# Output projection of a hybrid encoder layer: six of eight token groups as seven half-depth products of sums of quarters

## The chip, the cores and the metric

The kernel runs on one core of one Trainium2 chip. The metric is device microseconds of one execution. Three runs of the kernel before gave 2144.36, 2150.53 and 2152.09 us, so the median is 2150.53 us.

## The reference

One encoder layer with 2048 tokens and 1024 channels. A combined input projection feeds a gated DeltaNet and a stick-breaking attention; each branch is gated, projected up to 1024 channels and merged. What the change touches is the last line:

```python
merged = gates[..., :D_MODEL] * y_a + gates[..., D_MODEL:] * y_b      # [2048, 1024]
return x + jnp.einsum('bsd,de->bse', merged, w_out)                   # w_out: [1024, 1024]
```

All data is float32. The result is x plus a product of a 2048x1024 matrix with a 1024x1024 matrix.

## The kernel before

The program has two stages. `stage1` computes the input projection, the attention and the recurrence. `stage2` finishes the recurrence, computes the up projections (`up`, line 902) for eight groups of OG = 256 tokens, and then the output projection (`outs`, line 923) for the same eight groups.

Every product with f32r operands is made of three: each operand is split into a part `hi` (ScalarE casts it) and a rest `lo` (VectorE or GpSimd subtracts), and TensorE adds hi*hi, hi*lo and lo*hi (`mm3`, line 892). One matmul multiplies a stationary block of 128 channels by 128 tokens with 128 channels by 512 output columns.

`up(g)` leaves the merged activations in DRAM: for each of eight channel blocks VectorE multiplies two PSUM halves by the gates (`yt`, line 918), GpSimd adds the two (line 919), and the SP queue stores the block into the scratch `d_m[g]` (line 920), laid out as 128 channels, 8 blocks, 256 tokens.

`outs(g)` loads the eight blocks of `d_m[g]` back (`split`, line 882: tile `ot` with four buffers, ScalarE cast on line 888, VectorE subtract on line 889) into half of the tiles `xh2` and `xl2`, where the two halves alternate by group. For each of its two rows of 128 tokens it loads x (`xt`, three buffers), and for each of two halves of the output columns it issues 24 matmuls into one PSUM bank (tile `o`, pool `po`, six banks), adds x (line 933) and stores the row (line 937). The very last row is stored in two halves (line 935). That is 96 matmuls a group and 768 in all. The weights `w_out` lie in SBUF as hi and lo: blocks 0 to 3 in the pool `wq`, blocks 4 to 7 in the former space of x's third quarter of tokens (`xh3`, `xl3`).

The pools `oq` and `po` are opened on the right side of memory beside the pools `op` and `py` of the up projections, and a scheduler orders each engine's instructions and the SP queue's transfers. TensorE's own order is that of the program, held by explicit dependencies (`pin`, line 130). Each engine and the SP queue work through their lists in order, so an instruction that waits holds up what stands behind it.

Of the kernel before, what the change touches and what calls it, by code (L numbers as in the profile page):

```python
# [18 lines left out]
P = 128  # L19
# [18 lines left out]
class Block:  # L38
    """The layer in three stages; DRAM scratch carries what a stage leaves for a later one."""

    def __init__(self, ctx, tc, ins, out):
        self.ctx, self.tc, self.nc = ctx, tc, tc.nc
        self.i = ins
        self.out = out
        dr = ctx.enter_context(tc.tile_pool(name="dr", bufs=1, space=DRAM))

        def scratch(name, n, shape):
            return [dr.tile(shape, F32, name=f"{name}{i}") for i in range(n)]

        self.d_kq = dr.tile([NC, P, NH, 2, P], F32, name="d_kq")  # L50
        self.d_kt = dr.tile([NC, P, NH, P], F32, name="d_kt")
        self.d_vn = dr.tile([NC, P, NH, P], F32, name="d_vn")
        self.d_qk = dr.tile([NC, P, NH, P], F32, name="d_qk")
        self.d_mt = dr.tile([NC, NH, P, P], F32, name="d_mt")
        self.d_tt = dr.tile([NC, NH, 2, HB, HB], F32, name="d_tt")
        self.d_za = scratch("d_za", NC, [P, NH * P])
        self.d_q = dr.tile([2, SH * SD, S], F32, name="d_q")
        self.d_k = dr.tile([2, SH * SD, S], F32, name="d_k")
        self.d_v = dr.tile([SH, P, NT, P], F32, name="d_v")
        self.d_zb = scratch("d_zb", 4, [P, S])  # L60
        self.d_g = scratch("d_g", S // OG, [P, KB, 2, OG])
        self.d_oa = dr.tile([4, P, S], F32, name="d_oa")
        self.d_ob = dr.tile([4, P, S], F32, name="d_ob")
        self.d_m = dr.tile([S // OG, P, KB, OG], F32, name="d_m")
        self.now, self.pending, self.back, self.credit, self.rate = 0, [], None, 0.0, 0.0
        self.op, self.lead = None, 0
        self.chain, self.last, self.clock, self.attended, self.zb_done = False, None, 0.0, False, 0
        self.consts()
# [35 lines left out]
    def params(self):  # L104
        """The small parameters."""
# [24 lines left out]
    def pin(self, ins):  # L130
        """Keep the tensor engine in program order."""
        if self.chain and self.last is not None:
            self.tc.add_manual_dep(ins.ins, self.last, mybir.DependencyInfo(mybir.DependencyClass.NoSync, mybir.DependencyReason.DATA), reason="order")
        self.last = ins.ins.name if self.chain else None

    def load(self, *args):
        """A load whose queue keeps program order during the first tiles."""
# [6 lines left out]
    def defer(self, steps, fn):  # L144
        """Emit fn after the matrix products of `steps` further steps."""
        self.pending.append((self.now + steps, fn))
# [9 lines left out]
    def advance(self, amount, limit=4.0):  # L156
        """Let the background work emit about `amount` us of the tensor engine's time, or what it has ready."""
# [18 lines left out]
    def drain(self):  # L176
        """All that is left of the background work."""
        while self.back is not None:
            self.advance(1e9)
            self.clock += 0.2  # L180
# [13 lines left out]
    # ---------------------------------------------------------------- stage 1  # L194
# [63 lines left out]
    def ready(self, g):  # L258
        """Have the recurrence done for tokens of the up projections' group g."""
# [13 lines left out]
    def gap(self):  # L273
        """Background work between the products of a projection; the recurrence follows the attention."""
# [58 lines left out]
    def rsq(self, pool, ssq, n, scale, eps, tag):  # L333
        """(ssq * scale + eps) ** -0.5 on n columns."""
# [7 lines left out]
    def prep_x(self, first):  # L342
        """Normalised x, transposed to channels by tokens, in two parts that f32r products carry exactly."""
# [40 lines left out]
    def mm_chan(self, w, j, tg, between=None):  # L384
        """Projection block [128 channels, 512 tokens]."""
# [10 lines left out]
    def mm_tok(self, w, t, ps, n):  # L396
        """Projection block [128 tokens, n channels]."""
# [31 lines left out]
    def decays(self):  # L429
# [14 lines left out]
        # e = exp(-|xa|) = s1 / s2, log1p(e) = 2 atanh(e / (2 + e)), e / (2 + e) = s1 / (2 s2 + s1)  # L444
# [56 lines left out]
    def qkb_store(self, qn, dst, kind, u, tp):  # L501
        """To channels by tokens, q with both gains, in two parts that f32r products carry exactly."""
# [31 lines left out]
    def conv(self, ps, b, halo):  # L534
        """Causal four-tap convolution of a block; the caller multiplies what it returns for SiLU."""
# [36 lines left out]
    def qk_tok(self, kq, tg, h):  # L572
        """Norms of q and k, k by tokens, and the decay between a chunk's tokens."""
# [95 lines left out]
    # gated delta rule: within a chunk of 128 tokens, inverses of the two diagonal blocks of 64  # L669
    def dn_solve(self):  # L670
        """Unit triangular inverses by substitution, one block to a partition.

        With b[x, i] = -m[i, x] for x < i, step j adds b[x, j] b[j, i] to b[x, i]."""
# [38 lines left out]
    def dn_states(self):  # L712
# [9 lines left out]
        def store(most=0):  # L722
            """Emit what is due, and all but `most` of the rest when its time comes."""
# [55 lines left out]
    def dn_chunk(self, c, loads, st, mo):  # L779
        """One chunk of the recurrence; k and q come without their norms, which nk, nbr and rq carry."""  # L780
# [28 lines left out]
        # rms over a head's values; o carries neither q's norm nor dk ** -0.5 yet  # L809
# [21 lines left out]
    # ---------------------------------------------------------------- stage 2  # L831
    def stage2(self):
        """The up projections follow the recurrence; then the rest."""
        NO = S // OG
        with ExitStack() as ctx:
            self.op = ctx.enter_context(self.pool("op"))
            self.py = ctx.enter_context(self.pool("py", space=PSUM))
# [19 lines left out]
            self.oq = ctx.enter_context(self.pool("oq", side="right"))  # L857
            po = ctx.enter_context(self.pool("po", bufs=6, space=PSUM, side="right"))
            while jobs:
                self.run_job(jobs)  # L860
            for g in range(NO):
                self.outs(g, self.wo, po)

    def run_job(self, jobs):
        """A piece of the first job; the next one's loads run ahead of its end."""
# [16 lines left out]
    def split(self, src, k, g):  # L882
        """[128, OG] from DRAM in two parts, one of two sets."""
# [18 lines left out]
    def up(self, g):  # L902
        """Gated sum of both up projections for OG tokens, channels by tokens."""
# [19 lines left out]
    def outs(self, g, wo, po):  # L923
        nc, op = self.nc, self.op
        m = [self.split(self.d_m[g, :, k], k, g) for k in range(KB)]
        for t in range(OG // P):
            r0 = g * OG + t * P
            xt = self.oq.tile([P, D], F32, tag="xt", name="xt", bufs=3)
            nc.sync.dma_start(xt, self.i["x"][0, r0:r0 + P])
            for c in range(2):  # L930
# [3 lines left out]
                if r0 + P == S:  # L934
                    nc.sync.dma_start(self.out[0, r0:, c * TG:c * TG + TG], xt[:, c * TG:c * TG + TG])
            if r0 + P < S:
                nc.sync.dma_start(self.out[0, r0:r0 + P], xt)

    def att_pools(self, ctx):
# [9 lines left out]
        # added to a logit, it makes the key weigh nothing and break nothing  # L949
# [4 lines left out]
    # from a tile's products to its transposes, from there to the products with v, between two tiles, in us  # L954
    LT, LP, LZ = 4.5, 2.2, 1.3

    def attention(self):
        """Stick-breaking attention: one slot is a tile of 128 queries by 512 keys (or fewer on the diagonal)."""
# [5 lines left out]
        def ready():  # L964
            """Emit what is due; the sets of buffers bound how far one kind runs ahead of another."""
# [105 lines left out]
    def att_trans(self, A, m, edge):  # L1071
        """Two tiles' weights for two blocks of keys, the later block first, keys by queries in two parts."""
# [44 lines left out]
```

## Time and profile before

| what | value |
|---|---|
| runs of the kernel | 2144.36, 2150.53, 2152.09 us (median 2150.53) |
| profiled execution, span from first to last instruction | 2144.5 us |
| TensorE busy | 2058.2 us, 96% |
| VectorE busy | 1493.9 us, 70% |
| ScalarE busy | 875.2 us, 41% |
| GpSimd busy | 969.8 us, 45% |
| output projection, first to last matmul | 1963.4 to 2140.7 us |

The page gives the profiled execution's span and no other time for it; that span lies at the fastest of the three runs and 6.0 us under their median. Busy shares are of the whole span; an engine that is lightly loaded on average can be the last to arrive in one stage.

### The profile page before, as it was taken

The page shows a single profiled execution, that of the slowest core. Times are in us where ns is not written, and L with a number is a line of the kernel's source. Part 1 is how long each engine was busy: PE and PEld are TensorE (multiplying, and loading weights), DVE is VectorE, ACT ScalarE, POOL GpSimd, SP SyncE. Part 2 cuts the span into 40 slices and gives each one's busy share as a digit, 9 for nine tenths or more (in the row PEclk, how much of TensorE's full clock was granted, in tenths as well). Part 3 has the DMA queues.
Part 4 walks back from the last instruction along what each step waited for, and adds up shares of the span by engine and source line. Part 5 has one row for each costly group of instructions (what it writes and reads, how often), then busy time and mean ns, then how long its engine had stood idle before and what let it go on. Part 6 is the DMA issues. An engine that isn't in the chain of part 4 may idle for free.

```text
span 2144.5 us, 36573 instructions
## 1 busy us (share of the span) xinstructions
PE 2058.2 (96%) x12903; PEld 1821.1 (85%) x12903; DVE 1493.9 (70%) x2899; ACT 875.2 (41%) x1695; POOL 969.8 (45%) x820
## 2 busy tenths in 40 slices
PE   7999988999999999999999999999999999999999
PEld 7988767779999988878778888888788899999887
DVE  7367778887998329898889898889854466433221
ACT  6224433422222126666666666666643321211110
POOL 4335666534443215555556655555436655521000
PEclk9999999999999999999999999999999999999999
DMA  7123332226333553333664443333337787764442
GB/s 238 63 62 94 94 104 84 84 73 125 118 114 111 151 137 105 104 113 109 159 171 128 125 117 99 107 103 104 101 107 232 221 272 220 228 183 139 152 136 82
DMA packets 279702, 282.52 MB, mean 132 GB/s; under 512 B 49440, under 2 KB 215520, under 8 KB 279392
## 3 DMA queue, kind: packets, MB, share of 16 engines
q1 hardware_dynamic: 279520, 280.19, 44.8%
q8 instruction: 103, 1.69, 0.3%
q14 instruction: 79, 0.65, 0.1%
HBM read 177.35 MB, written 102.76 MB: 131 GB/s over the span
## 4 chain that ended last, share of the span: by engine, by line
PE 59%; DVE 23%; ACT 6%; DMA 4%; issue 4%; POOL 3%; SPq 0%; ACTq 0%; POOLq 0%; DVEq 0%
PE pj L124 30%; DVE r L1065 9%; PE o L124 8%; PE y L124 6%; DVE acc L548 4%; PE av L124 4%; DVE lo L1084 3%; PE at L128 3%; PE dn L124 3%; PE z L124 3%; ACT r L1061 2%; PE tp L128 1%; DMA wraw<-in_w_in_dram 1%; DVE halo L544 1%; DVE carry L1067 1%
## 5 line engine op out<-in xcount | busy, mean ns | idle before, releaser
L1068 POOL TENSOR_TENSOR s<-s,r 128x512 f32<-128x512 f32 (+2 forms) x320 | 372.5, 1174 | 335.5 <-DVE r L1065 183.7
L124 PE MATMUL pj<-xh,whi 128*128 128x512 f32 x1024 | 420.9, 411 | 12.0 <-ACT u L542 10.1
L124 PE MATMUL pj<-xh,wlo 128*128 128x512 f32 x1024 | 405.3, 396 | 0.0
L124 PE MATMUL pj<-xl,whi 128*128 128x512 f32 x1024 | 404.7, 395 | 0.0
L1065 DVE TENSOR_TENSOR_SCAN r<-r,carry,zero 128x512 f32<-128x512 f32 x192 | 302.2, 1574 | 23.2 <-ACT r L1061 22.0
L124 PE MATMUL pj<-whi,xh 128*128 128x256 f32 (+1 forms) x1024 | 293.3, 286 | 1.0 <-ACT xh L380 1.0
L124 PE MATMUL pj<-whi,xl 128*128 128x256 f32 (+1 forms) x1024 | 289.7, 283 | 0.0
L124 PE MATMUL pj<-wlo,xh 128*128 128x256 f32 (+1 forms) x1024 | 289.5, 283 | 0.2 <-DVE wlo L330 0.2
L124 PEld LDWEIGHTS pj<-xh,whi 128*128 128x128 f32 x1024 | 194.0, 189 | 49.2 <-ACT u L542 14.9
L1061 ACT ACTIVATE r<-z 128x512 f32<-128x512 f32 (+2 forms) x320 | 171.9, 537 | 152.2 <-PE z L124 53.9
L124 PEld LDWEIGHTS pj<-xh,wlo 128*128 128x128 f32 x1024 | 193.3, 189 | 44.5
L124 PEld LDWEIGHTS pj<-xl,whi 128*128 128x128 f32 x1024 | 194.3, 190 | 32.0
L1084 DVE TENSOR_TENSOR lo<-at,hi 128x512 fp32r<-128x512 f32 (+1 forms) x288 | 183.7, 653 | 28.3 <-ACT hi L1083 27.1
L124 PEld LDWEIGHTS pj<-whi,xh 128*128 128x128 f32 x1024 | 194.1, 190 | 1.4 <-ACT xh L380 1.4
L124 PEld LDWEIGHTS pj<-wlo,xh 128*128 128x128 f32 x1024 | 194.3, 190 | 0.5 <-DVE wlo L330 0.5
L124 PEld LDWEIGHTS pj<-whi,xl 128*128 128x128 f32 x1024 | 193.9, 189 | 0.3 <-DVE xl L381 0.3
L1083 ACT CAST hi<-at 128x512 fp32r<-128x512 f32 (+1 forms) x288 | 154.3, 571 | 96.7 <-PE at L128 94.7
L124 PE MATMUL z<-kt,qt 128*128 128x512 f32 (+3 forms) x640 | 189.4, 377 | 4.2 <-ACT s L1062 2.9
L330 POOL TENSOR_TENSOR wlo<-wraw,whi 128x512 fp32r<-128x512 f32 (+2 forms) x66 | 122.4, 1854 | 112.6 <-ACT whi L329 111.7
L1062 ACT ACTIVATE s<-z 128x512 f32<-128x512 f32 (+2 forms) x320 | 171.1, 535 | 0.0
L128 PE MATMUL at<-ident,s 128*128 128x128 f32 x1088 | 156.9, 274 | 11.3 <-POOL s L1068 11.1
L124 PE MATMUL av<-lo,vt 128*128 128x256 f32 x576 | 148.4, 292 | 17.0 <-DVE r L1064 9.9
(200 smaller groups left out, 4293.5 us busy)
## 6 DMA issues: line engine op xcount, KB each, us to landing
kt<-d_k SPq DMA_DIRECT2D x160, 128.0 KB, 3.0
vt<-d_v SPq DMA_DIRECT2D x80, 256.0 KB, 3.5
xt<-in_x_dram SPq DMA_DIRECT2D x32, 512.0 KB, 3.9
qt<-d_q SPq DMA_DIRECT2D x64, 256.0 KB, 5.2
d_g<-sg SPq DMA_DIRECT2D x128, 128.0 KB, 2.5
gt<-d_g SPq DMA_DIRECT2D x64, 256.0 KB, 3.6
wraw<-in_w_in_dram SPq DMA_DIRECT2D x56, 256.0 KB, 3.2
wraw<-in_w_in_dram SPq DMA_DIRECT2D x18, 512.0 KB, 3.8
```

What stands on the lines that cost most here:

```text
L124: self.pin(self.nc.tensor.matmul(out, lhsT, rhs, **kw))
L128: self.pin(self.nc.tensor.transpose(*args))
L330: (eng or nc.gpsimd).tensor_tensor(lo[:, ks, :n], raw[:, :, :n], hi[:, ks, :n].bitcast(F32), ALU.subtract)
L544: nc.vector.tensor_copy(halo, u[:, TG:TG + 3])
L548: nc.vector.scalar_tensor_tensor(acc, u[:, k:k + TG], self.tap(k, b), acc, ALU.mult, ALU.add)
L1061: nc.scalar.activation(r[:, :w], z[:, :w], AF.Sigmoid, scale=-(SD ** -0.5))
L1062: nc.scalar.activation(s[:, :w], z[:, :w], AF.Sigmoid, scale=SD ** -0.5)
L1065: nc.vector.tensor_tensor_scan(r[:, 0:w][:, ::-1], r[:, 0:w][:, ::-1], self.zero.to_broadcast([P, w]), init, ALU.mult, ALU.add)
L1067: nc.vector.tensor_copy(carry[i], r[:, 0:1])
L1068: nc.gpsimd.tensor_mul(s[:, :w], s[:, :w], r[:, 1:w + 1])
L1083: nc.scalar.copy(hi[:, c:], flat[:, c:])
L1084: nc.vector.tensor_tensor(lo[:, c:], flat[:, c:], hi[:, c:].bitcast(F32), ALU.subtract)
```

## The change

The up projections' pools are closed before the output projection starts, and the output projection's pools (`oq`, and `po` with seven banks) are opened in their place. Groups 0 and 1 are computed as before, except that each of the two `xt` tiles has one buffer of its own and the last row is stored whole. Between them `out_sums` loads `w_out` again, a quarter of its rows at a time, and forms four combinations of its quarters, the sums `t7`, with 16 subtractions of 128x512 on GpSimd and 16 splits into hi and lo. They lie where the weights of the up projections were (`xh0`, `xl0`, `xh1`, `xl1`).

Groups 2 to 7 use `outs7`. The group's activations are a 2x2 arrangement of quarters (two rows of 128 tokens, two halves of the channels): a11, a12, a21, a22. One transfer of 1 MB brings them into the tile `m`, which has one buffer and shares it with the tile of `out_sums` (tag `raw`). GpSimd forms four combinations s1 to s4 of 128x512 (the tiles are named `s0` to `s3`). Seven products of half depth (four channel blocks, 12 matmuls of 512 columns each) take the place of eight: p1 = a11*B11, p6 = s2*T2, p7 = s3*T3, p5 = s1*T1, then a12*B21 added into p1's bank, s4*B22 added into p5's bank, and p4 = a22*T4. Every left operand is split (`halves`: a ScalarE cast and a VectorE subtract of 128x512) into one of eight slots in `xh2` and `xl2`, taken in turn. VectorE forms u2 = p6 + p1 and u3 = p7 + u2; GpSimd adds u2 to one quarter of x and u3 to two; VectorE adds p1, p5 (twice) and p4 from PSUM.

```diff
     def stage2(self):
         with ExitStack() as ctx:
-            self.op = ctx.enter_context(self.pool("op"))
-            self.py = ctx.enter_context(self.pool("py", space=PSUM))
+            rest = ExitStack()
+            self.op = rest.enter_context(self.pool("op"))
+            self.py = rest.enter_context(self.pool("py", space=PSUM))
...
-            self.oq = ctx.enter_context(self.pool("oq", side="right"))
-            po = ctx.enter_context(self.pool("po", bufs=6, space=PSUM, side="right"))
             while jobs:
                 self.run_job(jobs)
-            for g in range(NO):
-                self.outs(g, self.wo, po)
+            rest.close()
+            self.op = self.oq = ctx.enter_context(self.pool("oq"))
+            po = ctx.enter_context(self.pool("po", bufs=7, space=PSUM))
+            self.outs(0, self.wo, po)
+            t7 = self.out_sums()
+            self.outs(1, self.wo, po)
+            for g in range(2, NO):
+                self.outs7(g, self.wo, t7, po)
...
+    def halves(self, hi, lo, src):
+        self.nc.scalar.copy(hi, src)
+        self.nc.vector.tensor_tensor(lo, src, hi.bitcast(F32), ALU.subtract)
+
+    def out_sums(self):
+        nc, oq = self.nc, self.oq
+        t7 = [[None] * 4 for _ in range(4)]
+        for k in range(4):
+            raw = oq.tile([P, KB * OG], F32, tag="raw", name="raw", bufs=1)
+            for r in range(2):
+                nc.sync.dma_start(raw[:, r * D:r * D + D], self.i["w_out"][0, (k + 4 * r) * P:(k + 4 * r) * P + P])
+            b11, b12, b21, b22 = (raw[:, TG * n:TG * n + TG] for n in range(4))
+            t = [oq.tile([P, TG], F32, tag=f"s{n}", name=f"s{n}", bufs=1) for n in range(4)]
+            for o, x, y in ((t[0], b12, b11), (t[1], b22, t[0]), (t[2], b22, b12), (t[3], b21, t[1])):
+                nc.gpsimd.tensor_tensor(o, x, y, ALU.subtract)
+            for n in range(4):
+                t7[n][k] = tuple(x[n // 2][:, n % 2 * 4 + k] for x in (self.xh, self.xl))
+                self.halves(*t7[n][k], t[n])
+        return t7
+
+    def outs7(self, g, wo, t7, po):
+        nc, oq = self.nc, self.oq
+        m = oq.tile([P, KB, OG], F32, tag="raw", name="m", bufs=1)
+        nc.sync.dma_start(m, self.d_m[g])
+        a11, a12, a21, a22 = (m[:, 4 * k:4 * k + 4, r * P:r * P + P] for r in range(2) for k in range(2))
+        s1, s2, s3, s4 = (oq.tile([P, 4, P], F32, tag=f"s{n}", name=f"s{n}", bufs=1) for n in range(4))
+        for o, x, y, op in ((s1, a21, a22, ALU.add), (s2, s1, a11, ALU.subtract), (s3, a11, a21, ALU.subtract), (s4, a12, s2, ALU.subtract)):
+            nc.gpsimd.tensor_tensor(o, x, y, op)
+        xt = [oq.tile([P, D], F32, tag=f"xt{r}", name="xt", bufs=1) for r in range(2)]
...
+        def product(ps, a, b, first=True):
+            slot = self.slot
+            self.slot = (slot + 1) % KB
+            hi, lo = (x[2][:, slot].rearrange("p (k t) -> p k t", k=4) for x in (self.xh, self.xl))
+            self.halves(hi, lo, a)
+            for k in range(4):
+                for n, (u, v) in enumerate(((hi, b[k][0]), (hi, b[k][1]), (lo, b[k][0]))):
+                    self.mm(ps, u[:, k], v, start=first and k == 0 and n == 0, stop=k == 3 and n == 2, skip_group_check=not first)
...
+        product(p1, a11, quarter(0, 0))
+        nc.scalar.copy(m1, p1)
+        product(p6, s2, t7[1])
+        add(nc.vector, u2, p6, m1)
+        product(p7, s3, t7[2])
+        add(nc.vector, u3, p7, u2)
+        add(nc.gpsimd, x22, x22, u3)
+        product(p5, s1, t7[0])
+        add(nc.vector, x22, p5, x22)
+        product(p1, a12, quarter(1, 0), False)
+        add(nc.gpsimd, x12, x12, u2)
+        add(nc.vector, x11, p1, x11)
+        product(p5, s4, quarter(1, 1), False)
+        add(nc.gpsimd, x21, x21, u3)
+        add(nc.vector, x12, p5, x12)
+        nc.sync.dma_start(self.out[0, rows[0]], xt[0])
+        product(p4, a22, t7[3])
+        add(nc.vector, x21, p4, x21)
+        nc.sync.dma_start(self.out[0, rows[1]], xt[1])
```

The SP queue at the end of the last up projection, before: `d_m` is the store of a block of the up projection, `gt` the load of its gates, and `ot` the load of activations for the output projection.

```order
L911 DMA gt<-d_g_93 128x512
L887 DMA ot<-d_m 128x256
L920 DMA d_m<-yt 128x256
L887 DMA ot<-d_m 128x256 x3
...
L920 DMA d_m<-yt 128x256 x3
L887 DMA ot<-d_m 128x256
L920 DMA d_m<-yt 128x256
L887 DMA ot<-d_m 128x256 x4
L920 DMA d_m<-yt 128x256
L887 DMA ot<-d_m 128x256 x3
```

The same place now, and the rows that follow up to the first load of a group's activations in one piece (`m`); `raw` is the second load of `w_out` and `xt` is x:

```order
L916 DMA gt<-d_g_93 128x512
L925 DMA d_m<-yt 128x256 x5
L892 DMA ot<-d_m 128x256 x4
L934 DMA xt<-in_x_dram 128x1024 x2
L892 DMA ot<-d_m 128x256 x4
L953 DMA raw<-in_w_out_dram 128x1024 x2
L892 DMA ot<-d_m 128x256 x8
L953 DMA raw<-in_w_out_dram 128x1024 x2
...
L953 DMA raw<-in_w_out_dram 128x1024 x2
L939 DMA out_dram<-xt 128x1024
L967 DMA m<-d_m 128x2048
```

All loads of groups 0 and 1 moved behind the last store of the up projections; before, all eight of group 0 and five of group 1 stood ahead of it.

GpSimd in one of the later groups (before, GpSimd has nothing behind the last `yt`); `s0`, `s2`, `s1`, `s3` with m_23297 are the sums s1, s3, s2, s4 of group 4, the last row begins group 5, and `xt_23175`, `xt_23176` are the x rows of group 3, where the first of the two additions to `xt_23176` is to the quarter that p5 also goes to:

```order
L971 TENSOR_TENSOR s0_23299<-m_23297 128x512
L971 TENSOR_TENSOR s2_23301<-m_23297 128x512
L971 TENSOR_TENSOR s1_23300<-s0_23299,m_23297 128x512
L994 TENSOR_TENSOR xt_23175<-xt_23175,u2_23181 128x512
L971 TENSOR_TENSOR s3_23302<-m_23297,s1_23300 128x512
L994 TENSOR_TENSOR xt_23176<-xt_23176,u3_23182 128x512 x2
L971 TENSOR_TENSOR s0_23431<-m_23429 128x512
```

VectorE beside it, in group 3; the tile o_23231 is p5's bank, o_23179 is p1's, o_23280 is p4's:

```order
L944 TENSOR_TENSOR xl2_141<-m_23297,xh2_137 128x512
L994 TENSOR_TENSOR u2_23181<-o_23198,m1_23180 128x512
L944 TENSOR_TENSOR xl2_141<-s2_23301,xh2_137 128x512
L994 TENSOR_TENSOR u3_23182<-o_23214,u2_23181 128x512
L944 TENSOR_TENSOR xl2_141<-s1_23300,xh2_137 128x512
L944 TENSOR_TENSOR xl2_141<-s0_23299,xh2_137 128x512
L944 TENSOR_TENSOR xl2_141<-m_23297,xh2_137 128x512
L994 TENSOR_TENSOR xt_23176<-o_23231,xt_23176 128x512
L994 TENSOR_TENSOR xt_23175<-o_23179,xt_23175 128x512
L944 TENSOR_TENSOR xl2_141<-s3_23302,xh2_137 128x512
L994 TENSOR_TENSOR xt_23175<-o_23231,xt_23175 128x512
L944 TENSOR_TENSOR xl2_141<-m_23297,xh2_137 128x512
```

A group's sums and splits are made one group ahead, and the x quarter that p5 goes to gets u3 on GpSimd behind five other sums.

## Rows read from the trace of the kernel before

**Rows 1.** The chain of waits in order of time, from 1955 us: start, length, what.
```profile
1955.00 8.40 PE y L124 x70
1963.40 177.30 PE o L124 x768
2140.70 0.02 issue
2140.72 0.69 DVE xt L933
```

**Rows 2.** Busy time by stretch: length, busy of five engines, TensorE clock, DMA share, GB/s.
```profile
1985.20:2007.00 21.80, 21.80 (x96) 17.71 (x95) 5.63 (x12) 2.75 (x7) 0.00 (x0) 1.00 0.42 142
2051.00:2073.00 22.00, 22.00 (x97) 17.87 (x96) 6.04 (x13) 3.52 (x9) 0.00 (x0) 1.00 0.44 143
```

**Rows 3.** Timelines at the up projections' end: start, length, engine, what, idle before.
```profile
1942.91 0.41 ACT L888 CAST xh<-ot 128x256 fp32r<-128x256 f32 x1 [4.07 <-DMA ot<-d_m]
1963.49 0.69 DVE L918 TENSOR_TENSOR yt<-y,gt 128x512 f32<-128x512 f32 x1 [0.16 <-issue]
1964.26 0.74 POOL L919 TENSOR_TENSOR yt<-yt 128x256 f32<-128x256 f32 x1 [1.89 <-DVE yt L918]
1965.72 0.39 SPq L920 DMA_DIRECT2D d_m<-yt  x1
```

**Rows 4.** DMA issues from 1964 to 2140 us: KB each, us to landing.
```profile
out_dram<-xt SPq DMA_DIRECT2D x15, 512.0 KB, 2.7
xt<-in_x_dram SPq DMA_DIRECT2D x13, 512.0 KB, 3.3
ot<-d_m SPq DMA_DIRECT2D x49, 128.0 KB, 2.8
out_dram<-xt SPq DMA_DIRECT2D x1, 256.0 KB, 2.0
```

**Rows 5.** All loads into `ot` from 1920 to 1990 us: time to landing.
```profile
DMA to landing us min/median/max: 2.4/2.9/4.6
```

**Rows 6.** Groups by line and shape, whole span: count, busy us, mean ns, idle before.
```profile
L888 ACT CAST xh<-ot 128x256 fp32r<-128x256 f32 x128 | 49.9, 406 | 241.4 <-PE o L124 101.1 <-PE y L124 77.9 <-DMA ot<-d_ob 29.2
L879 ACT CAST woh<-raw 128x512 fp32r<-128x512 f32 x8 | 5.0, 619 | 16.9 <-DMA raw<-in_w_out_dram 15.9 <-DMA gt<-d_g 0.8
L1084 DVE TENSOR_TENSOR lo<-at,hi 128x512 fp32r<-128x512 f32 x224 | 149.4, 683 | 27.9 <-ACT hi L1083 27.1
L933 DVE TENSOR_TENSOR xt<-o,xt 128x512 f32<-128x512 f32 x32 | 22.1, 690 | 114.5 <-PE o L124 114.5
```

**Rows 7.** GpSimd groups by line and shape, whole span.
```profile
L880 POOL TENSOR_TENSOR xl<-raw,xh 128x512 fp32r<-128x512 f32 x24 | 30.5, 1282 | 9.2 <-ACT xh L879 7.8 <-DMA vn<-d_vn 1.4
L1068 POOL TENSOR_TENSOR s<-s,r 128x512 f32<-128x512 f32 x224 | 300.2, 1350 | 257.1 <-DVE r L1065 123.3 <-DVE r L1064 40.6 <-ACT s L1062 26.1
L330 POOL TENSOR_TENSOR wlo<-wraw,whi 128x512 fp32r<-128x512 f32 x40 | 57.4, 1435 | 73.0 <-ACT whi L329 72.7
```

**Rows 8.** Timeline of VectorE and GpSimd where they meet, from 1937 us.
```profile
1937.79 1.98 DVE L889 TENSOR_TENSOR xl<-ot,xh 128x256 fp32r<-128x256 f32 x4
1937.82 0.99 POOL L919 TENSOR_TENSOR yt<-yt 128x256 f32<-128x256 f32 x1 [2.14 <-DVE yt L918]
1940.70 0.73 POOL L919 TENSOR_TENSOR yt<-yt 128x256 f32<-128x256 f32 x1 [1.89 <-DVE yt L918]
```

**Rows 9.** TensorE around a wait for VectorE: timeline rows, then two stretches.
```profile
1862.39 0.28 PE L124 MATMUL y<-xh,xl 128*128 128x256 f32 x1
1865.24 0.39 PE L124 MATMUL y<-xh,xh 128*128 128x256 f32 x1 [2.58 <-DVE yt L918]
...
1866.00:1869.40 3.40, 3.40 (x18) 3.40 (x18) 3.22 (x4) 2.11 (x6) 3.40 (x4) 0.51 0.82 255
1869.40:1871.00 1.60, 1.60 (x15) 1.60 (x15) 1.60 (x2) 0.84 (x2) 1.41 (x2) 1.00 0.93 316
```

More of the change, by code (lines that the diff above doesn't have):

```diff
@@ L65, in __init__ @@
         self.now, self.pending, self.back, self.credit, self.rate = 0, [], None, 0.0, 0.0
-        self.op, self.lead = None, 0
+        self.op, self.lead, self.slot = None, 0, 0
         self.chain, self.last, self.clock, self.attended, self.zb_done = False, None, 0.0, False, 0
@@ L927, in outs @@
             r0 = g * OG + t * P
-            xt = self.oq.tile([P, D], F32, tag="xt", name="xt", bufs=3)
+            xt = self.oq.tile([P, D], F32, tag=f"xt{t}", name="xt", bufs=1)
             nc.sync.dma_start(xt, self.i["x"][0, r0:r0 + P])
@@ L933, in outs @@
                 nc.vector.tensor_tensor(xt[:, c * TG:c * TG + TG], ps, xt[:, c * TG:c * TG + TG], ALU.add)
[L934 to L937, printed above, removed]
+            nc.sync.dma_start(self.out[0, r0:r0 + P], xt)
+    def halves(self, hi, lo, src):
+        self.nc.scalar.copy(hi, src)
+        self.nc.vector.tensor_tensor(lo, src, hi.bitcast(F32), ALU.subtract)
@@ new lines, in outs7, with bank, temp @@
+    def outs7(self, g, wo, t7, po):
[7 more added lines that the diff above has]
+        xt = [oq.tile([P, D], F32, tag=f"xt{r}", name="xt", bufs=1) for r in range(2)]
+        rows = [slice(g * OG + r * P, g * OG + r * P + P) for r in range(2)]
+        for r in range(2):
+            nc.sync.dma_start(xt[r], self.i["x"][0, rows[r]])
+        (x11, x12), (x21, x22) = ((t[:, 0:TG], t[:, TG:D]) for t in xt)
+        quarter = lambda k, c: [tuple(u[:, c * TG:c * TG + TG] for u in w) for w in wo[4 * k:4 * k + 4]]
+        def product(ps, a, b, first=True):
[6 more added lines that the diff above has]
+                    self.mm(ps, u[:, k], v, start=first and k == 0 and n == 0, stop=k == 3 and n == 2, skip_group_check=not first)
+        def bank():
+            return po.tile([P, TG], F32, tag="o", name="o")
+        def temp(name):
+            return oq.tile([P, TG], F32, tag=name, name=name, bufs=1)
+        add = lambda eng, o, x, y: eng.tensor_tensor(o, x, y, ALU.add)
+        p1, m1, u2, u3 = bank(), temp("m1"), temp("u2"), temp("u3")
+        product(p1, a11, quarter(0, 0))
+        nc.scalar.copy(m1, p1)
+        p6 = bank()
+        product(p6, s2, t7[1])
+        add(nc.vector, u2, p6, m1)
+        p7 = bank()
+        product(p7, s3, t7[2])
+        add(nc.vector, u3, p7, u2)
+        add(nc.gpsimd, x22, x22, u3)
+        p5 = bank()
+        product(p5, s1, t7[0])
[7 more added lines that the diff above has]
+        nc.sync.dma_start(self.out[0, rows[0]], xt[0])
+        p4 = bank()
+        product(p4, a22, t7[3])
+        add(nc.vector, x21, p4, x21)
+        nc.sync.dma_start(self.out[0, rows[1]], xt[1])
```

## The prediction, made before the changed kernel ran

> **What bounds the kernel now.** I read the chain of waits first, because it says which engine a saved instruction must come from. From 1963.4 us to 2140.7 us it is one piece: 768 matmuls of the output projection on TensorE, with a VectorE addition behind it [rows 1]. So a matmul taken away there shortens the span by its spacing, 177.30 / 768 = 0.2309 us, as long as TensorE keeps being fed. The table by stretches says how much room the others have: in 22 us TensorE is busy throughout at full clock, VectorE for about 6, ScalarE for about 3, GpSimd not at all, and the DMA engines are at 42 to 44% [rows 2]. What the change adds goes to those engines, so the averages look harmless. What matters is order: who must finish before TensorE may go on. For that I read the timelines at the start of the stage [rows 3], the DMA landing times [rows 4, 5] and the durations of the kinds of instruction that are added [rows 6, 7].
>
> All times below are counted on the profiled execution, whose span is 2144.5 us; the median of the runs is 2150.53 us, 6.0 more, and I carry the difference over to the median. About 0.5%, 10.75 us, is what a measurement of this kernel can tell from no change.
>
> **The change part by part.**
>
> 1. *Fewer matmuls.* Six groups have 84 instead of 96: 72 x 0.2309 = 16.6 us less. The forms are the same 128x512, the weights stay in SBUF, so nothing else about a matmul changes.
>
> 2. *The way in.* Before, the activations of group 0 were split by 1945 us, long before TensorE needed them at 1963.4: the row at 1942.91 is the fifth of its eight casts [rows 3]. Now the first load stands behind the last store of the up projections. That store waits for GpSimd's last addition, which ends at 1964.26 + 0.74 = 1965.0 [rows 3]. One issue takes 0.4, so the first load is issued at 1965.4, lands 2.8 later [rows 4], and is cast in 0.41 [rows 6]: the first matmul starts at about 1968.6 instead of 1963.4, 5.2 us late. There are four buffers, so the fifth load waits for VectorE's first subtract (about 0.5, a quarter of the 1.98 in [rows 8]): issued 1969.1, ready 1972.3, while the first four blocks keep TensorE until 1968.6 + 12 x 0.2309 = 1971.4. That adds 0.9. Together **+6.1**. With the shortest and longest landing seen, 2.4 and 4.6 [rows 5], twice in a row, it is 5.3 to 9.7.
>
> 3. *The clock.* After a wait of 2.58 us at 1865 us TensorE ran at 1.2 GHz for 3.4 us: 18 matmuls took 3.40 us where at 2.4 GHz 15 took 1.60 [rows 9]; so 18 would have taken 1.9, and the loss was 1.5. A wait of 5.2 us should bring the same: **+1.6**; 0 if the low level passes while TensorE stands idle, 3.4 if it comes twice.
>
> 4. *The sums of w_out,* cover and price. Sixteen GpSimd subtractions run under groups 0 and 1. If one takes c, a round is a load of 3.3 [rows 4], 0.2 of issue and 4c, and the single buffer keeps rounds from overlapping. The first load is issued behind the eighth load of group 0, at about 1971.0. After four rounds comes group 2's 1 MB load. No row shows such a load: 128 KB lands in 2.8 and 512 KB in 3.3 [rows 4], a slope that gives 4.0, and two of 512 KB one after the other would be 6.6; I take 5, nearer the first, since the DMA engines are half idle. For c the rows of the same shape say 1.28 with little beside it, 1.35 in the attention and 1.435 for the subtraction in the projections [rows 7]. I take 1.44, as here too VectorE subtracts beside it. Then rounds end at 1971.0 + 4 x 9.26 = 2008.0, m is there at 2013.1, and the sum for p6 with its cast at 2013.1 + 3 x 1.44 + 0.62 = 2018.0. TensorE reaches p6 at 1963.4 + 6.1 + 1.6 + 192 x 0.2309 + 2.77 = 2018.2. So **0**, with 0.2 to spare; what is late next, if this gives way, is p6 itself.
>
> 5. *The wait for p5's bank in group 2.* The fifth and sixth products add into banks that VectorE and ScalarE read first. The sixth may start only when p5 has been added to x, and that addition waits for GpSimd's x + u3, which in GpSimd's list stands behind the next group's first three sums and x + u2; those wait for the next 1 MB load. Its issue needs group 2's fourth sum: 2013.1 + 4 x 1.44 = 18.9, then 0.4 + 5, five GpSimd operations 7.2 and VectorE 0.69 [rows 6]: 2032.2. TensorE wants the bank five products after 2015.4, at 2029.3: **+2.9** (0 with c = 1.28 and a fast load, 5 with c = 1.74).
>
> 6. *The ring in groups 3 to 6.* The same steps close a circle: load 5, six GpSimd operations 6c, VectorE 0.69, the sixth product 2.77, the cast of a22 0.62, two VectorE operations 1.4, issue 0.4. At c = 1.44 that is 19.5 against a group's 84 x 0.2309 = 19.4: **+0.4** over four groups. Splits (ScalarE 7 x 0.62, VectorE 13 x 0.69 a group) are made a group ahead and lie beside TensorE; without that cover each would cost 1.3 before its product.
>
> 7. *The end.* The last store is a whole row: 2.7 instead of 2.0 [rows 4], **+0.7**. The loads of x have one buffer a row now, and each waits for its row's store, 2.7 + 3.3 = 6 us into the next group, before u3 exists: nothing.
>
> Sum: -16.6 + 6.1 + 1.6 + 0 + 2.9 + 0.4 + 0.7 = -4.9 us; 2150.5 - 4.9 = **2145.6**.
>
> **Rivals.** *GpSimd sets the pace (the slower side).* In terms 4 to 6 c counts 19, 6 and 24 times: a tenth of a microsecond more in c costs 4.9 us. The gain is gone at c = 1.54, and it is slower by 10.75 from c = 1.76. For it: GpSimd's 256-column addition took 0.99 beside four VectorE subtracts from SBUF and 0.73 alone [rows 8]; the same stretch on 1.28 gives 1.74, hence -4.9 + 49 x 0.30 = +9.8, **2160**. The Trainium skill says the same of the cause: by its page "GPSIMD Engine Reference", section "Key points", GpSimd shares its SBUF interfaces with VectorE and contends with VectorE instructions that have two SBUF inputs, as all the added splits have; the rows at 1937 agree in sign. Against it: in the attention, with VectorE scanning beside it, the mean was 1.35, and the splits fill only 2.8 of some 8 us of a group's GpSimd work. Chance 0.22, of which 0.08 beyond c = 1.76.
>
> *The loads set the pace.* If 1 MB lands in 6.6, because the row stores and x loads travel with it, term 4 costs 1.4, term 5 1.6 more and the ring 6.4: +4.5, **2155**. For it: one buffer, so each load starts only when the last reader is done; against it: 42% DMA share. Chance 0.13.
>
> *The waits are mostly covered.* Shortest landing, c = 1.28, no low clock, loads of 4.0: -16.6 + 5.3 + 0.7 = -10.6, **2140**. For it: GpSimd is otherwise idle here. Against it: the way in stands in the order and can't be avoided, and the wait of 2.58 did bring the low clock. Chance 0.10, half of it beyond 0.5%.
>
> **The numbers.** The forecast, 2145.6, has 0.55 and its own range is 2142 to 2151. The rivals reach from 2140 to 2160; leaving out the upper part of the first, the lower edge of the last and some of the scatter of 8 us between runs, I give 2139.5 to 2159. Faster by over 0.5%: half of the last rival and the forecast's lower edge, 0.08. Slower by over 0.5%: 0.09, the first rival from c = 1.76 on and a little for the loads. Same: 0.83.
>
> **What would show it.** Right: 696 matmuls of the output projection; TensorE idle for 5 to 6 us from 1963.4, ended by a load or cast of group 0, and a granted clock of half for some 3 us behind it; p6 of group 2 waiting under 2 us; VectorE's addition of p5 waiting for GpSimd in group 2; groups 3 to 7 at 19.4 to 19.6 us each. Wrong: groups of 20 us or more with TensorE waiting for VectorE each time (the ring, then c or the landing says which), a start of group 2 later than 2020 us, or no wait at all at 1963 us.

## The result and the profile after the change

The changed kernel took 2168.93 us (median of four runs, 2165.81 to 2171.85) where the kernel before, on the same chip, took 2148.62 (2144.36 to 2152.09). The ratio is 1.0097 with a 95% interval of 1.0081 to 1.0114: slower by about 20 us, outside the predicted range. The profiled span is 2164.9 us against 2144.5.

The 72 matmuls are gone, which saves 16.6 us, and the kernel is 20 us slower, so some 37 us of waiting and of low clock have come in. The chain of waits of the changed kernel, from the up projections' end, answers to [rows 1] (start, length, what):

```profile
1966.30 5.19 DMA ot<-d_m
1973.81 5.92 DMA raw<-in_w_out_dram
...
2019.02 4.74 DMA m<-d_m
2023.89 1.28 POOL s L971
...
2029.01 2.38 DVE xl L944 x2
2031.45 5.93 DMA m<-d_m
...
2048.02 4.61 PE o L124 x12
2054.01 6.02 DMA m<-d_m
...
2135.73 24.89 PE o L124 x108
```

Before, this stretch was one TensorE row of 768 matmuls. Now the end is set by loads, GpSimd's sums and VectorE's splits in turn, and TensorE enters the chain only in places, mostly for a single product; the last nine products run unbroken. TensorE's waits in the stage, by what ended them (total, times, longest):

```profile
PE o L124 <- DVE xt L994: 10.1, 5, 3.3
PE o L124 <- ACT xh L893: 6.6, 2, 5.5
PE o L124 <- ACT xh L943: 5.9, 1, 5.9
PE o L124 <- DVE xl L944: 2.5, 1, 2.5
```

And where they stand in TensorE's timeline (start, length, what, idle before it):

```profile
1963.52 0.28 PE L124 MATMUL y<-xh,xl 128*128 128x256 f32 x1
1969.28 0.80 PE L124 MATMUL o<-woh,xh 128*128 128x512 f32 x1 [5.48 <-ACT xh L893]
1972.05 0.80 PE L124 MATMUL o<-woh,xh 128*128 128x512 f32 x1 [1.12 <-ACT xh L893]
...
1974.35 0.63 PE L124 MATMUL o<-woh,xl 128*128 128x512 f32 x1
1974.78 0.63 PE L124 MATMUL o<-woh,xh 128*128 128x512 f32 x1
...
1977.34 0.46 PE L124 MATMUL o<-xh,xh 128*128 128x512 f32 x1
...
2024.53 0.79 PE L124 MATMUL o<-woh,xh 128*128 128x512 f32 x1 [5.94 <-ACT xh L943]
...
2032.64 0.79 PE L124 MATMUL o<-xh,xl 128*128 128x512 f32 x1 [2.52 <-DVE xl L944]
```

Behind the longer waits the matmuls start 0.43 us apart (1974.35 to 1974.78) instead of 0.2309. The table by stretches shows why, as in [rows 9]; the columns are those of [rows 2]:

```profile
1969.20:1977.40 8.20, 7.00 (x16) 4.98 (x17) 2.37 (x6) 1.89 (x6) 0.00 (x0) 0.50 0.81 265
2049.10:2052.60 3.50, 3.50 (x10) 2.72 (x9) 0.69 (x1) 0.41 (x2) 0.00 (x0) 0.51 0.00 0
```

The granted clock is 0.50, that is 1.2 GHz, after the wait at the way in, and again at 2049.1 after a wait for p5's bank.

With the starts of matmuls as marks the loss divides in three. The row at 1977.34 is the stage's 16th matmul and the row at 2032.64 the 207th, p6's third in group 2. The 108 matmuls in the last row of the chain end at 2160.62, and the last of them starts 0.40 earlier, at 2160.22.

| stretch | length | at 0.2309 a matmul | lost | predicted |
|---|---|---|---|---|
| way in, 1963.52 to 1977.34 | 13.82 | 15, 3.46 | 10.4 | 7.7 (terms 2, 3) |
| to p6 of group 2, 2032.64 | 55.30 | 191, 44.10 | 11.2 | 0 (term 4) |
| to the last matmul, 2160.22 | 127.58 | 489, 112.91 | 14.7 | 3.3 (terms 5, 6) |

The costliest groups from 1960 us on (as in [rows 6, 7]: count, busy us, mean ns, idle before):

```profile
L944 DVE TENSOR_TENSOR xl<-s,xh 128x512 fp32r<-128x512 f32 x40 | 45.6, 1149 | 20.7 <-ACT xh L943 19.4
L994 POOL TENSOR_TENSOR xt<-xt,u 128x512 f32<-128x512 f32 x18 | 29.1, 1630 | 13.5 <-DVE u L994 11.7 <-DMA xt<-in_x_dram 1.9
L944 DVE TENSOR_TENSOR xl<-m,xh 128x512 fp32r<-128x512 f32 x18 | 22.3, 1240 | 22.7 <-ACT xh L943 22.7
L971 POOL TENSOR_TENSOR s<-m 128x512 f32<-128x512 f32 x12 | 17.9, 1516 | 55.8 <-DMA m<-d_m 55.8
L957 POOL TENSOR_TENSOR s<-raw 128x512 f32<-128x512 f32 x8 | 12.1, 1514 | 29.5 <-DMA raw<-in_w_out_dram 29.5
```

GpSimd's operations took 1.55 us on average over all 58, from 1.44 to 1.71 by kind (term 4 took 1.44), which is some way towards the first rival. What none of the prediction's cases held is VectorE: the splits priced at 0.69 took 1.15 and 1.24. The timelines of the two engines show them meet, first in `out_sums`, then in group 2:

```profile
1984.13 1.47 POOL L957 TENSOR_TENSOR s<-raw,s 128x512 f32<-128x512 f32 x1
...
2002.89 1.29 POOL L957 TENSOR_TENSOR s<-raw 128x512 f32<-128x512 f32 x1 [4.37 <-DMA raw<-in_w_out_dram]
...
2005.51 1.74 POOL L957 TENSOR_TENSOR s<-raw 128x512 f32<-128x512 f32 x1
2004.87 5.46 DVE L944 TENSOR_TENSOR xl<-s,xh 128x512 fp32r<-128x512 f32 x4 [4.37 <-ACT xh L943]
...
2026.81 1.73 POOL L971 TENSOR_TENSOR s<-s,m 128x512 f32<-128x512 f32 x1
2028.62 1.61 POOL L971 TENSOR_TENSOR s<-m,s 128x512 f32<-128x512 f32 x1
...
2027.32 1.77 DVE L944 TENSOR_TENSOR xl<-m,xh 128x512 fp32r<-128x512 f32 x1
2030.70 0.68 DVE L944 TENSOR_TENSOR xl<-m,xh 128x512 fp32r<-128x512 f32 x1
```

GpSimd's subtraction at 2002.89 takes 1.29 with nothing on VectorE beside it; the one at 2005.51 runs beside two of the four splits that begin at 2004.87 (their row counts short waits for casts between them) and takes 1.74. VectorE's split at 2027.32 runs beside GpSimd's sums and takes 1.77; the one at 2030.70 starts after GpSimd's last sum ended at 2030.23 and takes 0.68. Landing times, as in [rows 4]:

```profile
m<-d_m SPq DMA_DIRECT2D x6, 1024.0 KB, 6.1
raw<-in_w_out_dram SPq DMA_DIRECT2D x8, 512.0 KB, 4.9
```

The term took 5 for the 1 MB load and 3.3 for w_out. Last, the SP queue's timeline:

```profile
1969.72 4.04 SPq L892 DMA_DIRECT2D ot<-d_m  x4
1973.81 0.90 SPq L953 DMA_DIRECT2D raw<-in_w_out_dram  x2
1976.16 11.95 SPq L892 DMA_DIRECT2D ot<-d_m  x8
1988.16 0.90 SPq L953 DMA_DIRECT2D raw<-in_w_out_dram  x2
...
2019.02 0.33 SPq L967 DMA_DIRECT2D m<-d_m  x1
```

The first round lasts 14.35 us: its load takes 5.92 by the chain above, GpSimd is done with its last sum at 1984.13 + 1.47 = 1985.6, and the next load is issued only at 1988.16, because it stands behind eight loads of group 1 in the queue, which wait for buffers that VectorE's splits free. Two of those splits, from 1982.93 on beside GpSimd's sums, took 1.51 each, where the kernel before took 0.43 on average. The other three rounds last 10.3 on average.

### The profile page after: what moved, and what is told of

It is laid out like the page before. It is cut to its first block, busy times and chain, and to the rows that moved or that the text cites. A ratio compares the mean times of both kernels' runs of the same rounds, so it can differ in the third digit from the quotient of the medians.

```text
span 2164.9 us, 36460 instructions
## 1 busy us (share of the span) xinstructions
PE 2051.9 (95%) x12831; PEld 1813.4 (84%) x12831; DVE 1545.4 (71%) x2921; ACT 893.9 (41%) x1711; POOL 1058.4 (49%) x878
## 4 chain that ended last, share of the span: by engine, by line
PE 56%; DVE 22%; DMA 7%; ACT 6%; issue 5%; POOL 4%; SPq 0%; ACTq 0%; POOLq 0%; DVEq 0%
PE pj L124 31%; DVE r L1146 9%; PE y L124 7%; DVE acc L548 4%; PE av L124 4%; PE dn L124 4%; PE at L128 3%; DVE lo L1165 3%; PE z L124 3%; PE o L124 2%; DMA raw<-in_w_out_dram 2%; DMA wraw<-in_w_in_dram 1%; PE tp L128 1%; ACT r L1142 1%; DMA m<-d_m 1%
## 5 line engine op out<-in xcount | busy, mean ns | idle before, releaser
L124 PE MATMUL pj<-xh,whi 128*128 128x512 f32 x1024 | 419.7, 410 | 12.0 <-ACT u L542 10.1
```

The costliest lines, as they stand in the source:

```text
L124: self.pin(self.nc.tensor.matmul(out, lhsT, rhs, **kw))
```

## The experiments

Four questions: what the way in costs alone, whether the sums' engine matters, what the shared bank of p5 and s4's product costs, and whether the loads alone would do the same. Ratios are to the kernel before, run beside each on the same chip (medians 2147.08, 2146.70 and 2146.88 for the three sets, which end with the fourth, the eighth and the tenth experiment). "Stage" is the time from the last up-projection matmul's start to that of the last matmul; it was 177.18 before and 196.70 after, and 160.5 is what 696 matmuls would need at 0.2309 each. The end of the up projections varied from 1959.9 to 1966.8 among the profiled runs, which no run here explains; the stage leaves that out.

**1. The pools alone.** Eight groups of eight products in the changed pools, no sums.

```diff
-            self.outs(0, self.wo, po)
-            t7 = self.out_sums()
-            self.outs(1, self.wo, po)
-            for g in range(2, NO):
-                self.outs7(g, self.wo, t7, po)
+            for g in range(NO):
+                self.outs(g, self.wo, po)
```

> The changed pools with eight products in all eight groups: no sums of w_out, no seven-product groups. Theory A (the way in is dear: in the changed kernel TensorE stood 5.5 and 1.5 us at the start of the stage and ran 7 us of work at the low clock, some 3.3 us lost): about 10 us over the kernel before, near 2159, with a wait of 5 to 6 us on group 0's cast and half clock behind it. Theory B (the way in is as cheap as predicted, 6 to 8 us, and the rest of the loss lies in the sums): 2155 to 2157. Theory C (moving the pools costs nothing by itself): within 2 us of the kernel before.

2155.33 us (2151.56 to 2161.43), ratio 1.0041 (1.0021 to 1.0061): 8.3 us for the way in by itself, near terms 2 and 3 (7.7), but the interval reaches from 4.5 to 13.1 us, and the profiled run, the slowest of the six, has a stage 11.1 us longer. Either way the way in cannot explain 20.

**2. An early way in.** The loads of `ot` and x get a pool of their own beside the up projections, so they no longer wait for the last store.

```diff
+            self.oi = ctx.enter_context(self.pool("oi", side="right"))
             while jobs:
                 self.run_job(jobs)
             rest.close()
-            self.op = self.oq = ctx.enter_context(self.pool("oq"))
+            self.oq = ctx.enter_context(self.pool("oq"))
+            self.op = self.oi
...
-            xt = self.oq.tile([P, D], F32, tag=f"xt{t}", name="xt", bufs=1)
+            xt = self.oi.tile([P, D], F32, tag=f"xt{t}", name="xt", bufs=1)
...
```

> The changed kernel, but the tiles for the activations of groups 0 and 1 and for x lie in a pool of their own that is opened beside the up projections', so their loads stand ahead of the last stores again. Theory A: the waits at 1963 us (7 us) and the low clock behind them (3.3 us) go, and w_out's second load is issued some 8 us earlier too, so group 2's wait does not grow: 8 to 11 us less than the changed kernel, near 2159. Rival (the sums of w_out set when group 2 starts and are not moved): TensorE only waits longer at group 2, within 3 us of the changed kernel.

2153.52 (2148.40 to 2159.11), ratio 1.0033 (1.0020 to 1.0047). No wait is left at the start of the stage; yet TensorE still waited 5.0 us and 1.8 us in group 2 and 9.3 in five waits for p5's bank. About 15 us came back of the changed kernel's 20, where 8 to 11 were expected. The profiled runs show why: they differ by 13.2, of which the stage, now 186.11, gives 10.6, as expected, and an earlier end of the up projections 3.7, while 1.1 is lost behind the last matmul. The chain of sums moved with the way in: counted from the last up-projection matmul, the first `raw` load came 8.0 us earlier (at 1962.14 instead of 1973.81).

**3. The sums on VectorE.** All 40 sums move from GpSimd to VectorE; loads, buffers and products stay.

```diff
-                nc.gpsimd.tensor_tensor(o, x, y, ALU.subtract)
+                nc.vector.tensor_tensor(o, x, y, ALU.subtract)
...
-            nc.gpsimd.tensor_tensor(o, x, y, op)
+            nc.vector.tensor_tensor(o, x, y, op)
```

> The changed kernel with the sums of w_out and of the activations on VectorE in place of GpSimd (16 and 4 a group); GpSimd keeps the additions to x. Theory contention (GpSimd's sums of 1.3 to 1.75 us and VectorE's splits of 1.2 to 1.8 us slow each other): the sums take 0.7 us, the splits 0.7, a round of w_out goes from 10.4 to about 8.5 us, group 2's wait of 6 us goes to under 1, the waits for p5's bank shrink from 2 to under 1 us: 12 to 18 us less, 2151 to 2157. Rival loads (the loads of 4.9 and 6.1 us set the rounds and the ring): rounds stay over 9.5 us and the waits for the bank stay above 1.5 us, 2163 or more. Rival VectorE (17 more operations of 0.7 us a group make it the bound): over 2169.

2149.91 (2144.13 to 2152.79), ratio 1.0016 (1.0004 to 1.0029): 19 us less than the changed kernel by the medians, 18.1 by the stage, though VectorE has 40 operations more. The groups show why:

```profile
L944 DVE TENSOR_TENSOR xl<-s,xh 128x512 fp32r<-128x512 f32 x40 | 28.8, 736 | 0.0
L944 DVE TENSOR_TENSOR xl<-m,xh 128x512 fp32r<-128x512 f32 x18 | 14.2, 787 | 0.0
L957 DVE TENSOR_TENSOR s<-raw 128x512 f32<-128x512 f32 x8 | 5.5, 690 | 6.0 <-DMA raw<-in_w_out_dram 6.0
```

The same splits are back at 0.74 and 0.79, and 28 of the sums take 0.69 (the other twelve, the last two of each group, 0.87 and 1.42 on average). In the changed kernel VectorE spent 67.9 us on 58 splits; here it spends 43.0 on them and 32.5 on the 40 sums, 7.6 more in all, and GpSimd's 60.7 us of sums are gone. The wait for group 2's activations is gone; what stays is one wait of 5.3 for p5's bank in group 2, which was 3.3 in the changed kernel and was expected to fall under 1, three short ones, and the way in. The scheduler also moved two of the eight loads of group 1 behind the second `raw` load, so the first round, 10.5 instead of 14.35, is not the engine's doing alone.

**4. A bank of its own for s4's product.** One more VectorE addition from PSUM; nothing else changes.

```diff
-        product(p5, s4, quarter(1, 1), False)
+        p3 = bank()
+        product(p3, s4, quarter(1, 1))
         add(nc.gpsimd, x21, x21, u3)
         add(nc.vector, x12, p5, x12)
+        add(nc.vector, x12, p3, x12)
```

> The changed kernel, but the sixth product (s4) goes to a bank of its own instead of p5's, with one more VectorE addition a group, so TensorE no longer waits until p5 has been added to x. Theory bank (that wait, 12.2 us over five groups and some 3 us of low clock behind it, is a wait of its own): 10 to 15 us less, 2154 to 2159, groups 3 to 6 at about 19.4 us. Rival ring (the load of the next group's activations closes the circle in another place, at the split of a22 or of s2): the waits move to ScalarE's or VectorE's splits, under 4 us gained.

2149.81 (2143.53 to 2152.25), ratio 1.0011 (0.9998 to 1.0024). Its chain of waits has a single TensorE row from group 2 on:

```profile
2031.61 113.48 PE o L124 x490
```

490 matmuls at 0.2316: with the extra bank, slow sums and 6 us loads hide completely behind TensorE from there on. So the loss of the whole third stretch, terms 5 and 6, hung on that bank; the stage is 15.5 us shorter, where 10 to 15 were expected. The 6.7 + 2.0 at group 2 and the 6.0 at the way in stay.

**5. to 7. Combinations.** Early way in and extra bank; the same with all sums on VectorE; the same with only the sums of w_out on VectorE. The edits are those above.

> The early way in and the own bank for the sixth product together. If the way in (about 15 us in the runs of its own), the bank (about 19) and the rest are separate waits, their gains add but for the part of the low clock that both counted: 2134 to 2140, under the kernel before by 7 to 13 us; what is left is group 2's wait for the sums of w_out, 5 to 7 us with its low clock. Rival (each only uncovers the next wait of the same ring): 2145 to 2150, no better than either alone.

2139.45 (2137.28 to 2145.98), ratio 0.9972 (0.9961 to 0.9982). What is left is group 2: 4.8 and 2.7 us.

> As the early way in with the own bank, and all sums on VectorE. Theory contention: rounds of w_out fall to about 8.3 us, group 2's activations arrive before TensorE is done with group 1, VectorE's 18 operations of 0.7 us fit into a group's 19.4: 2130 to 2135, near the full saving of 16.6 less 0.7 under the kernel before. Rival VectorE: its list in order (sums of the next group in front of the additions from PSUM that TensorE's banks wait for) brings back waits of 2 us and more in most groups: 2140 or more.

2127.27 (2126.87 to 2133.37), ratio 0.9916 (0.9898 to 0.9935): faster than both kernels. The stage takes 160.32, no more than 696 matmuls need. The one wait that the table of waits still shows:

```profile
PE o L124 <- DVE xl L946: 1.0, 1, 1.0
```

> As the early way in with the own bank, and only the 16 sums of w_out on VectorE; the sums of activations stay on GpSimd. Theory (group 2's late start is the rounds of w_out, and the groups behind have room once the bank is free): group 2's wait falls from 5 to about 2 us or less, groups 3 to 7 at 19.4: 2130 to 2136. Rival loads (rounds are the loads' 4.5 to 5 us): rounds above 9.5 us and a wait of over 4 us at group 2.

2134.72 (2131.25 to 2140.10), ratio 0.9947 (0.9926 to 0.9967). TensorE's stage is as short, 159.85, and the kernel still 7.5 us longer. Of the 7.3 between the two profiled runs, 2.2 are a later end of the up projections, and 5.6 lie behind the last matmul. The end of the chain of waits says where:

```profile
2115.51 4.99 DMA out_dram<-xt
2120.51 3.23 DMA xt<-in_x_dram
2123.90 1.27 POOL xt L996
```

x has one buffer a row. Group 7's load waits for group 6's store, and GpSimd's addition begins at 2123.90, after TensorE's last matmul at 2122.15. Term 7 put these loads at nothing, "6 us into the next group"; that holds only while a group's additions are not late themselves.

**8. No low clock at the way in and at group 2.** In the changed kernel 23 and 24 matmuls into an unread bank fill most of TensorE's two long waits.

```diff
...
+            warm(23)
             self.outs(0, self.wo, po)
             t7 = self.out_sums()
             self.outs(1, self.wo, po)
+            warm(24)
...
```

> The changed kernel with 23 matmuls more in front of group 0 and 24 in front of group 2, 5.3 and 5.5 us of TensorE's time into a bank that nobody reads, so that it works while it would have waited. Theory clock (the waits cost more than their length, since TensorE runs at 1.2 GHz behind them): group 0 and group 2 start as late as in the changed kernel but at full clock, 4 to 8 us less, 2161 to 2165. Rival (low clock comes whatever TensorE does there, or the waits hide it): within 2 us of the changed kernel, or more by what the added matmuls push back.

2166.69 (2165.96 to 2170.11), ratio 1.0096 (1.0081 to 1.0112), the ratio of the changed kernel. The clock did change: from 2018 to 2036 us the mean granted clock was 0.98, in the changed kernel 0.72. At the way in the first twelve matmuls ran at full clock, but a wait of 2.86 us followed them, with a clock of 0.52 from 1977 to 1980 behind it. p6's third matmul started 69.11 us after the last up-projection matmul, in the changed kernel 69.12. So the theory that the low clock costs time by itself missed: up to there it lies under the wait for the sums and costs nothing.

**9. No sums at all.** Each split reads a plain quarter, so the sums are left out and the output is not the layer's.

```diff
-            for o, x, y in ((t[0], b12, b11), ...):
-                nc.gpsimd.tensor_tensor(o, x, y, ALU.subtract)
+            t = [b11, b12, b21, b22]
...
-        s1, s2, s3, s4 = (oq.tile(...) for n in range(4))
-        for o, x, y, op in (...):
-            nc.gpsimd.tensor_tensor(o, x, y, op)
+        s1, s2, s3, s4 = a21, a11, a22, a12
```

> The changed kernel without its 40 GpSimd sums: each split reads a plain quarter of w_out or of the activations instead of a combination, so the sums of quarters are left out and the output is not the reference's; loads, buffers, splits, products and additions stay as they are. Theory A (the sums on GpSimd, and what they do to VectorE beside them, set the pace): VectorE's splits fall from 1.15 to about 0.7 us, a round of w_out lasts about 8 us instead of 10 to 14, p6 of group 2 starts within 2 us of when TensorE gets there (55 to 57 us after the up projections), the waits for p5's bank are under 1 us each; what is left is the way in, 8 us: 2147 - 16.6 + 8 + 2 = 2140, between 2137 and 2144. Theory B (the single buffers and their loads set the pace): a load only starts when the last split of the buffer is done, so TensorE still waits more than 4 us at group 2 and over 1 us in each later group: 2150 to 2160.

2143.24 (2134.85 to 2148.32), ratio 0.9977 (0.9962 to 0.9992). The single buffers are still there, and the loads land no faster (5.8 for 1 MB, 5.2 for w_out), yet TensorE waits only at the way in and 3.1 us in four waits for p5's bank, two of them over the 1 us expected:

```profile
PE o L124 <- ACT xh L893: 6.2, 1, 6.2
PE o L124 <- DVE xt L991: 3.1, 4, 1.4
...
L944 DVE TENSOR_TENSOR xl<-m,xh 128x512 fp32r<-128x512 f32 x42 | 30.3, 746 | 23.5 <-ACT xh L943 23.5
```

The splits of `raw` took 0.69. So the loads alone do not set the pace, and without GpSimd's sums VectorE's splits are at their price. From the first `raw` load to group 2's load it took 33.3 us here and 45.2 in the changed kernel. The 12 us are the sums, what they slow down, and a changed queue: the scheduler put four loads of group 1, not eight, ahead of the second `raw` load, and the wait in the queue in the changed kernel was 2.6.

**10. Early way in and sums on VectorE, one bank as in the change.**

> Early way in and all sums on VectorE, but the fifth and sixth products still share a bank: the version that was fastest so far without its extra bank. Theory A (the order of VectorE's list holds that bank in group 2 whenever the way in is): a wait of 5 to 6 us for p5's bank in group 2 and about 1 us behind it stay, the way in's 8 us go: about 2149.9 - 8 = 2142, against 2127.3 with the extra bank. Theory B (that wait was only the late loads of w_out): with the loads 11 us earlier it is gone too, and the extra bank is worth nothing here: 2127 to 2130.

2139.28 (2138.10 to 2142.54), ratio 0.9962 (0.9948 to 0.9977), 12 us more than with the extra bank:

```profile
PE o L124 <- DVE xt L996: 7.9, 4, 6.1
```

The wait of 6.1 in group 2 stays though the first `raw` load starts 6.6 us earlier than in experiment 3, counted from the last up-projection matmul (2.29 behind it instead of 8.92). In the chain of waits group 3's 1 MB load lands first, and VectorE then works without a break through group 3's sums and splits to p5's addition to x, which ends at 2025.6. The bank of experiment 6 removes the wait. That the order of VectorE's list makes it is read from the chain; a sum of 1.78 and two splits of 1.7 beside GpSimd's additions to x have their part in it.

Left open: two buffers for the 1 MB load were not tried. No run separates GpSimd's own pace (1.29 for a sum alone, where VectorE takes 0.69) from what the two engines lose side by side. And the fastest version gains 2.5 us beyond the stage's own 16.9; its up projections ended 3 us earlier (1960.15 against 1963.11), which the runs do not explain.

## Why the prediction was wrong, by its steps

**Terms 1 and 2 held, term 3 was too small.** The matmuls are 696, and where TensorE is fed they cost the same: the last 108 take 24.89, 0.2305 each. The way in cost 5.48 + 1.12 = 6.6 of waiting (6.1 predicted) and 3.8 besides, the low clock of 15 matmuls (1.6 predicted and at most 3.4, from a stretch in the kernel before that was half as long); alone it measured 8.3. This low clock did not decide the result: group 2 waited for the sums (experiment 8). The tail of term 7 is 0.5 (0.7 predicted).

**Term 4 failed first: "So 0, with 0.2 to spare".** p6 could go on at 2032.64 instead of 2018.0, 14.6 us late:
- 2.8: the first `raw` load was issued at 1973.81, not at 1971.0; the four loads ahead of it, waiting for buffers, held the queue for 4.04 from 1969.72.
- 8.2: four rounds took 45.2 instead of 37.0. Of that 5.1 is the first round: 2.6 is the hold in the SP queue, nearly all of the rest is a load of 5.92 instead of 3.3. The term let the rounds follow one another and left out what stood between them in the queue, though the order printed ahead of the prediction shows those eight loads. The other three rounds are 1.0 longer each, by the load and by sums at 1.74.
- 3.6: from the load of `m` to p6's third matmul 13.6 instead of 10.0. The 1 MB load itself was on time (4.74). But p6's split was the seventh piece of VectorE's list for the group, behind the splits of a11, s1, a12, s3 and a22 and an addition, the first four of them at 1.2 to 1.8 us each. p6's sum was cast by 2029.2, and VectorE came to it only at 2031.9. The term followed GpSimd and one cast and had no VectorE in it.

**Terms 5 and 6 failed by size.** The mechanism, p5's bank held until x gets p5, was right, and experiment 4 shows that it was the whole of it; 3.3 was predicted and 14.7 came: 10.1 of waits, and about 4.4 of low clock, 22 matmuls at 0.43 behind the waits that ended at 2032.64, 2048.02 and 2091.98. In group 2 the next 1 MB load did not wait for GpSimd's fourth sum, as term 5 has it (done at 2030.23), but for VectorE's split of a22, done at 2031.4, and was issued at 2031.45, 12 us later than predicted. From one issue of the 1 MB load to the next it took 21.1 to 22.6 us, where 19.5 were predicted: the load 6.1 instead of 5 (+1.1), GpSimd's six operations 9.4 by their means instead of 8.6 (+0.8), and where the wait brought the low clock the sixth product 4.61 instead of 2.77. The slope between two smaller loads, which gave 4.0, did not reach that far. The Trainium skill's page "DMA: Bandwidth & Descriptors", section "Measured (HBM→SBUF, 128 partitions, SWDGE, issued from GpSimd)", gives 6.15 us for 1 MB, for loads issued from GpSimd and without the time of issuing them. The six loads of this trace, issued from the SP queue, come near it: 6.1 by the median from issue to landing, and 4.74 for the first. Two of the signs of being wrong came true: group 2 began at 2024.53, and its successors took 21 to 23 us each, with TensorE waiting for VectorE each time.

**The first rival had the direction, not the price.** It stretched GpSimd alone. At the mean c of 1.55 of the 58 operations, 49 us for each us gives 49 x 0.11 = 5.4, so 2151.0 instead of 2168.9. The rest came from what ran beside it: splits at 1.7 times their price, the lists of VectorE and the SP queue, the landing times, and the low clock behind the longer waits. Its argument against itself, that the splits fill "only 2.8 of some 8 us" of GpSimd's work, used the unstretched duration of the very instructions that stretch. **The loads as the pace** are out as the whole cause by experiment 9 and by experiment 4, where 5.7 us loads hide behind TensorE. And the waits and the low clock do not add to the sums' delay: until group 2, whichever chain is longer counts (experiment 8).

## What to carry to other kernels

When work goes to an idle engine beside a busy one, look for rows where the two run side by side and price both engines at those durations, or move the work onto the busy engine and see whether the sum is shorter: here 40 sums cost less on VectorE than beside it. Where a buffer is reused within a group (here a PSUM bank), walk the in-order list of each engine up to the instruction that frees it, and ask first for a second buffer: one more bank and one more addition hid the same slow sums entirely from group 2's p6 on. A chain of loads must be walked in the queue's own order, with every foreign transfer that stands between two of its links.

## What was not expected of the hardware

Two engines slow each other by different shares. GpSimd's 128x512 float32 subtraction took 1.29 us alone and up to 1.74 beside VectorE's splits, most often one of these two values; VectorE's split took 0.68 alone and up to 1.77 beside GpSimd, so VectorE lost more. With the sums gone, and ScalarE's casts and the loads still there, the splits were back at 0.69 and 0.75 (experiment 9). In the prediction only the engine that the rows at 1937 show slowing [rows 8] was stretched.

The low clock came back after a wait of 1.83 us that ended at 2091.98, and not after waits of 1.62 and 1.39 in the groups beside it. But it also stayed away after a wait of 1.88 us, so here the length of a wait alone does not tell:

```profile
2091.98 0.50 PE L124 MATMUL o<-xh,xh 128*128 128x512 f32 x1 [1.83 <-DVE xt L994]
2094.00:2097.00 3.00, 3.00 (x9) 2.32 (x8) 0.77 (x2) 0.62 (x1) 0.00 (x0) 0.51 0.00 0
...
2135.73 0.50 PE L124 MATMUL o<-xh,xh 128*128 128x512 f32 x1 [1.88 <-DVE xt L994]
2138.00:2141.00 3.00, 3.00 (x15) 2.49 (x14) 1.29 (x2) 0.62 (x1) 0.00 (x0) 1.00 0.23 94
```

After the 1.83 the granted clock was still 1.00 from 2092 to 2093 and 0.51 from 2094 to 2097; after the 1.88 it was 1.00 from 2138 to 2141, and the last 108 matmuls ran at 0.2305 each. The prediction had the low clock only behind waits of 2.58 and more. But where another chain set the next start, full clock in its place bought nothing (experiment 8).
